# A forgetting-attention and SSD layer: the second query tile's causal mask added by GpSimd, norm sums taken as columns

## The chip, the cores and the metric

The kernel runs on one core of one Trainium2 chip. The metric is device time in microseconds (us), the median of several executions. The engines go by TensorE (PE, its weight loads PEld), VectorE (DVE), ScalarE (ACT), GpSimd (POOL) and SyncE (SP, which issues most transfers). Each takes its instructions in order; they meet at semaphores.

## The reference

One decoder layer for 1024 tokens and 1024 channels in fp32, 16 heads of 64 in either branch:

```
proj = RMSNorm(x) @ w_in -> z_ssm, xBC, dt, q, k, v, f, z_att, g_ssm, g_att
A: xBC -> causal conv, silu -> SSD scan in chunks of 128 -> y
   yg = y * silu(z_ssm);  yg *= rsqrt(mean(yg^2 over the 256 channels of a group) + eps)
B: per head, for each block of 128 queries
   s = q.k / sqrt(64) + F[query] - F[key],   F = cumsum(log sigmoid(f))
   s = -inf where key > query;  o = softmax(s) @ v;  o *= silu(z_att)
merged = sigmoid(g_ssm) * (A @ w_branch_ssm) + sigmoid(g_att) * (B @ w_branch_att)
out = x + RMSNorm(merged @ w_out)
```

Two places matter here: the causal mask in B, and the sum of squares over a group's 256 channels in A.

## The kernel before, in words

Tokens stand in tiles of 128 (`P`), eight of them, in two halves of 512 (`HALF`). The big projections are one long `Stream`: pairs of 128-column units are multiplied in seven products in place of eight (a Strassen-like scheme); every operand is split in a high and a low part so that three fast products make one near fp32. One product into one PSUM bank is 12 matmuls of 512 columns, cut in two half-steps of six. The rest of the program calls `stream.halves(n)` to place half-steps between its own work, so that TensorE has projections to stream while other engines work; a generator that yields n has n half-steps put behind that part (`stream.beside`).

**State-space stage.** `ssd(g)` runs for each of 4 groups over 8 chunks. `squares(g, ch, ...)` takes the norm's sum of squares for half `ch`: both channel tiles are multiplied with the gate, squared by ScalarE, added by VectorE into `zs[0]`. Lines 977 to 991 then split that sum in a high and a low part (`sqp`), let TensorE multiply both with a matrix of ones (`pv`: each row holds the sums of 512 tokens), copy one row (`line`), and turn it in four matmuls into four columns `pc`, which VectorE copies to `rc`. Half 0 is done inside the scan of the same group (`early`, from chunk 4 on), half 1 in `gate_and_norm`, which goes on to take the root, turn `rc` into rows, write them to DRAM (L1012), read them back broadcast as `r` (L1015), scale `xs` (L1022) and store it (L1027).

**Attention.** 8 pairs of heads `hp`, six steps `g` each (`GROUPS`, L1355): query tiles 7, 6 on the far keys and on the near keys, 5, 4 likewise, 3, 2 and 1, 0 on the near keys. In a step `scores(hp, g, u)` runs for both query tiles (u = 0, 1). It makes `s` for both heads e: three products, the heads side by side in the upper and lower half of the array. VectorE's reduction (L1511) writes s + F into `ex` and its minimum (signs are turned) into `nm`; ScalarE's exponential (L1515) works in place and sums up. `turned` then transposes `ex` on TensorE, copies the results to `p` (L1552, L1554), and `weighted` multiplies with v in the next step.

F of the keys is loaded broadcast as `fb` (L1372), for all 128 queries. A diagonal block needs the mask. For the odd query tiles (u = 0) `mask` adds `far`, 1e30 above the diagonal, to 128 columns of `fb` in place, on GpSimd (L1379, two instructions of 64 partitions and 2 x 128 columns). For the even ones (u = 1), whose keys in `fb` the other query tile needs unmasked, TensorE adds it: `corner`, two products with a shifted identity `eye` for either head, at the end of the score block (L1499). A score block of an even tile has 384 or 128 columns, so that in `ex[:, e, 1]` the columns 384 to 511 are unused in those steps; in steps 1 and 3 they hold scores.

The order of pinned instructions (`pin`, `mm`, `turn`) is that of the program, engine by engine; the others are placed by a planner that simulates the program, with `tc.high_priority()` ahead. One pass of the loop at L1691 is one step: scores of both tiles, `weighted` of the step before, half-steps (`ahead`), gates' loads, `loads(m)` (transfers of the coming steps and the masks of `fb`), `turned`, half-steps (`behind`).

Of the kernel before, what the change touches and what calls it, by code (L numbers as in the profile page):

```python
# [8 lines left out]
F32 = mybir.dt.float32  # L9
# [7 lines left out]
P = 128  # L17
# [69 lines left out]
def hybrid_layer(ctx: ExitStack, tc, a, out):  # L87
# [746 lines left out]
    def ssd(g):  # L834
# [108 lines left out]
        for c in range(NT):  # L943
# [11 lines left out]
            if c == 4:  # L955

                z, sq = (sp.tile([P, T + 4], F32, tag="u", bufs=2, name=n) for n in ("z", "sq"))
                sq = sq.bitcast(F32R)
                early = squares(g, 0, [z[:, half(j)] for j in range(2)], [sq[:, half(j)] for j in range(2)], z[0:1, 0:HALF])
                next(early)  # L960
# [5 lines left out]
    def squares(g, ch, zs, sqp, line):  # L966
# [26 lines left out]
    def gate_and_norm(g):  # L993
        xs = [groups[g][f"xs{j}"] for j in range(2)]

        def flat(tag, bufs, name):
            return sp.tile([P, 4, P], F32, tag=tag, bufs=bufs, name=name).rearrange("p a b -> p (a b)")

        yield from squares(
            g, 1, [flat("csb", 2, "z") for _ in range(2)], [flat("m4", 2, "sqp").bitcast(F32R) for _ in range(2)],  # L1000
            flat("ce", 1, "line")[0:1],
        )
# [289 lines left out]
    with tc.tile_pool(name="ssm", bufs=1, reuse_waits="tile", side="right") as sp, tc.tile_pool(  # L1292
        name="ssmp", bufs=1, space=PSUM, reuse_waits="tile", side="right"
    ) as pp:
        onesr = sp.tile([P, P], F32R, name="onesr")
        ones = onesr.bitcast(F32)
# [36 lines left out]
    with tc.tile_pool(name="att", bufs=1, reuse_waits="tile", side="right") as ap, tc.tile_pool(  # L1333
# [8 lines left out]
        nc.vector.memset(big[:, 0:192], -NEG)  # L1342
        for e in range(2):
            nc.vector.tensor_copy(eye[rows[e], 64:P], ident[rows[e], rows[e]])
            nc.gpsimd.affine_select(
                beyond[:, 192 * e : 192 * e + 192], big[:, 0:192], [[1, 192]], ALU.is_gt, 0.0, base=64 * e - 64,
                channel_multiplier=-1,
            )
            nc.vector.tensor_copy(far[rows[e], :], beyond[rows[e], 192 * e : 192 * e + 192])

        corner = [(eye[:, 64:192], far[:, 64:192]), (eye[:, 0:P], far[:, 0:P])]
# [22 lines left out]
        def mask(hp, i):  # L1374

            f = fb[hp, i // 4][:, :, i % 4 * P : i % 4 * P + P]
            for e in range(2):
                c = far[rows[e], 64 - 64 * e : 192 - 64 * e].unsqueeze(1).to_broadcast([64, 2, P])
                pin(nc.gpsimd.tensor_tensor(f[rows[e]], f[rows[e]], c, ALU.add))  # L1379
# [102 lines left out]
        def scores(hp, g, u):  # L1482
# [8 lines left out]
            diagonal = h == i // 4 and u  # L1491
            for m, (x, y) in enumerate(ops):
                for e in range(2):
                    mm(
                        s[e][:, 0:w], x[rows[e]], y[rows[e]], start=(m == 0), stop=(m == 2 and not diagonal),
                        skip_group_check=True,
                    )
            if diagonal:
                for n, (x, y) in enumerate(corner):  # L1499
                    for e in range(2):  # L1500
                        mm(
                            s[e][:, w - P : w], x[rows[e]], y[rows[e]], start=False, stop=(n == 1),
                            skip_group_check=True,
                        )
# [294 lines left out]
```

## Time and profile before

| | |
|---|---|
| runs | 1275.56, 1275.94, 1270.34 us; median 1275.56 |
| the profiled execution | 1276.93 us, span 1275.2 us, mean granted TensorE clock 0.998 |
| busy share of the span | PE 98%, PEld 77%, DVE 80%, ACT 62%, POOL 25% |
| first to last score matmul | 683.7 to 1109.3 us |
| mask matmuls L128 s<-far,eye | 128, 9.8 us busy, 222 ns each (matmuls overlap) |
| masks on GpSimd L1379 | 64, 49.5 us busy |
| norm sums: L977, L984 on ACT, L978 on DVE, pv and pv_t on PE | 8 of each, 16 and 32 matmuls |

A row of the profile gives engine, line, operation, what is written and read (out<-in, buffer numbers left out), partitions x columns and type, and xcount. Matmuls all have L128 and transposes L131, the lines of two helpers: they are told apart by their tiles. L1511 shows as `CUSTOM_DVE_ANT_0` and a short `DVE_READ_ACCUMULATOR2_ANT`, which writes the minimum. Ends of matmuls are modelled, and a matmul's duration (0.39 us for 512 columns) is longer than the distance to the next, so lengths are taken from start to start. In a timeline a row holds neighbouring instructions of one kind, and what stands in square brackets is the engine's idle time before it.

### The profile page before, as it was taken

To read this page: it belongs to the slowest core of one execution; us is meant where nothing else is said; L and a number is where in the kernel's file an instruction comes from. 1 tells how busy PE (TensorE), PEld (TensorE's weight loads), DVE (VectorE), ACT (ScalarE), POOL (GpSimd) and SP (SyncE) were. 2 spreads that over 40 slices of the span, in tenths; PEclk is the share of its full clock that TensorE was granted. 3 is DMA by queue.
4 is the path that set the end of the run, shared out by engine and by line. 5 is a ranking of instruction groups with operands and counts; after the bars stand their busy time and mean duration, and the time that the engine had idled before them with its cause. 6 is when DMAs were issued, how large, how long until landed. Compare 5 with 4: busy or idle time off the path is not lost.

```text
span 1275.2 us, 20797 instructions
## 1 busy us (share of the span) xinstructions
PE 1245.2 (98%) x6912; PEld 981.9 (77%) x6912; DVE 1016.0 (80%) x2001; ACT 793.6 (62%) x1735; POOL 319.5 (25%) x321
## 2 busy tenths in 40 slices
PE   5999999999999999999999999999999999999997
PEld 3688878788888888888887777777777777678886
DVE  7998896888888978997767667767789667797975
ACT  7745665556665765566555666666687666743753
POOL 4000440013400241114102123313112222256062
PEclk9999999999999999999999999999999999999999
DMA  8232452646336533744447576666687657766933
GB/s 294 72 125 73 147 164 87 186 153 195 119 116 206 173 131 111 223 151 134 137 154 255 167 225 200 215 222 217 226 296 273 204 197 244 236 202 212 367 115 100
DMA packets 152235, 233.56 MB, mean 183 GB/s; under 512 B 15200, under 2 KB 60736, under 8 KB 152128
## 3 DMA queue, kind: packets, MB, share of 16 engines
q1 hardware_dynamic: 136064, 196.08, 47.9%
q10 hardware_dynamic: 10560, 18.06, 3.7%
q0 software_dynamic: 5504, 18.09, 3.7%
q8 instruction: 54, 0.88, 0.3%
q14 instruction: 53, 0.43, 0.1%
HBM read 162.99 MB, written 72.34 MB: 185 GB/s over the span
## 4 chain that ended last, share of the span: by engine, by line
PE 80%; DVE 7%; DMA 6%; ACT 4%; issue 2%; SPq 0%; POOL 0%; DVEq 0%; ACTq 0%; POOLq 0%
PE pb L128 33%; PE pc L128 20%; PE pd L128 6%; PE av L128 5%; PE pt L131 5%; PE s L128 5%; PE yps L128 2%; DVE wop L351 1%; DVE sum L356 1%; DMA xt<-in_x 1%; DMA raw<-in_wu 1%; DMA rb<-st_dram 1%; PE st L128 1%; PE tr_v L131 1%; ACT wop L350 1%
## 5 line engine op out<-in xcount | busy, mean ns | idle before, releaser
L350 ACT ACTIVATE wop<-sum 128x512 fp32r<-128x512 f32 x180 | 112.5, 626 | 110.8 <-DVE sum L356 51.2
L351 DVE TENSOR_TENSOR wop<-sum,wop 128x512 fp32r<-128x512 f32 x180 | 137.0, 762 | 53.8 <-ACT wop L350 52.5
L1515 ACT ACTIVATE ex<-ex,nm 128x512 f32<-128x512 f32 (+1 forms) x192 | 116.2, 606 | 75.2 <-DVE nm L1511 74.9
L410 ACT ACTIVATE s<-pb 128x512 f32<-128x512 f32 x143 | 84.7, 592 | 93.4 <-PE pb L128 91.3
L128 PE MATMUL pb<-x0h,wop 128*128 128x512 f32 x384 | 131.6, 399 | 0.0
L351 DVE TENSOR_TENSOR wop<-raw,wop 128x512 fp32r<-128x512 f32 x144 | 106.6, 742 | 31.1 <-ACT wop L350 30.7
L128 PE MATMUL pc<-x2h,wop 128*128 128x512 f32 x384 | 130.3, 398 | 1.1 <-DVE u L425 1.1
L128 PE MATMUL pc<-x3h,wop 128*128 128x512 f32 x384 | 129.8, 396 | 1.1 <-DVE th L423 0.7
L128 PE MATMUL pb<-x4h,wop 128*128 128x512 f32 x384 | 129.1, 395 | 0.0
L128 PE MATMUL pb<-x6h,wop 128*128 128x512 f32 x376 | 126.8, 395 | 1.3 <-ACT s L410 1.3
L128 PE MATMUL pb<-x5h,wop 128*128 128x512 f32 x376 | 127.1, 395 | 0.0
L1511 DVE CUSTOM_DVE_ANT_0 ex<-s,fb 128x512 f32<-128x512 f32 (+1 forms) x192 | 96.8, 552 | 19.9 <-PE s L128 14.6
L350 ACT ACTIVATE wop<-raw 128x512 fp32r<-128x512 f32 x144 | 89.7, 623 | 15.6 <-PE pd L128 6.2
L128 PE MATMUL pd<-x1h,wop 128*128 128x512 f32 x288 | 96.3, 394 | 0.0
L128 PEld LDWEIGHTS pc<-x2h,wop 128*128 128x128 f32 x384 | 72.1, 188 | 18.6 <-issue 2.4
L128 PEld LDWEIGHTS pc<-x3h,wop 128*128 128x128 f32 x384 | 72.1, 188 | 18.2 <-issue 1.6
L128 PEld LDWEIGHTS pb<-x0h,wop 128*128 128x128 f32 x384 | 72.7, 189 | 17.3 <-issue 2.7
L128 PEld LDWEIGHTS pb<-x4h,wop 128*128 128x128 f32 x384 | 72.1, 188 | 16.7 <-issue 1.9
L128 PEld LDWEIGHTS pb<-x6h,wop 128*128 128x128 f32 x376 | 70.6, 188 | 18.1 <-ACT s L410 1.7
L211 POOL TENSOR_TENSOR wd<-wd 128x256 f32<-128x256 f32 x32 | 33.0, 1032 | 202.7 <-DMA wd<-in_wo 138.5
L128 PEld LDWEIGHTS pb<-x5h,wop 128*128 128x128 f32 x376 | 70.6, 188 | 16.7 <-issue 2.0
L128 PE MATMUL pc<-x3l,wop 128*128 128x512 f32 x192 | 75.1, 391 | 1.5 <-DVE x3l L279 1.5
(325 smaller groups left out, 3004.1 us busy)
## 6 DMA issues: line engine op xcount, KB each, us to landing
raw<-in_wu SPq DMA_DIRECT2D x128, 256.0 KB
csb<-cs_dram SPq DMA_DIRECT2D x32, 256.0 KB
q<-q_dram SPq DMA_DIRECT2D x32, 256.0 KB
k<-k_dram SPq DMA_DIRECT2D x16, 512.0 KB
fb<-f_dram SPq DMA_DIRECT2D x16, 512.0 KB
rb<-st_dram SPq DMA_DIRECT2D x48, 128.0 KB
wd<-in_wo SPq DMA_DIRECT2D x40, 128.0 KB
xt<-in_x SPq DMA_DIRECT2D x8, 512.0 KB
```

Of the source, the lines that this page charges most:

```text
L128: return tc.keep_in_program_order(nc.tensor.matmul(*args, **kw))
L131: return tc.keep_in_program_order(nc.tensor.transpose(out_, in_, idn))
L211: pin(nc.gpsimd.tensor_tensor(t[out_], t[a_], t[b_], ALU.subtract))
L350: nc.scalar.activation(op[:, 0], src, AF.Copy)
L351: nc.vector.tensor_tensor(op[:, 1], src, op[:, 0], ALU.subtract)
L356: self.adds.tensor_tensor(t, x, y, ALU.add)
L410: nc.scalar.activation(s, ps, AF.Copy)
L1511: nc.vector.tensor_tensor_reduce(o, s[e][:, 0:w], fb[hp, h][:, e, 0:w], 1.0, 3.0e38, ALU.add, ALU.min, nm)
L1515: pin(nc.scalar.activation(o, o, AF.Exp, scale=-1.0, bias=nm, accum_out=hd.at(hd.sm, i, h, e)))
```

## The change

In the state-space stage the sum of squares is not split. TensorE takes each 128 tokens of `zs[0]` as weights and multiplies a single column of ones, in plain fp32: four matmuls give the four columns at once. The row, its copy, its four turns and one `yield 2` go; so do the tiles for the parts and the row. `ones` is plain fp32.

In the attention `eye`, `corner` and the mask matmuls go. `far` is 128 x 128. `mask` takes one head at a time (128 partitions, 128 columns) and can write its sum elsewhere: for the even query tiles to `spare`, the unused quarter of `ex`. The reduction of tiles 6 and 2 is split in two: all but the last 128 columns against `fb`, then the last 128 against `spare`, starting from the minimum `na` of the first; tiles 4 and 0 have 128 columns only, and take theirs against `spare` in one instruction. The masks for `spare` are issued after `turned` in steps 1 and 3 (for tiles 4 and 2), in `loads` of step 4 (tile 0) and of step 5 (tile 6 of the next heads).

```diff
-    def squares(g, ch, zs, sqp, line):
+    def squares(g, ch, zs):
...
         nc.vector.tensor_tensor(zs[0], zs[0], zs[1], ALU.add)
-        nc.scalar.activation(sqp[0], zs[0], AF.Copy)
-        nc.vector.tensor_tensor(sqp[1], zs[0], sqp[0], ALU.subtract)
         yield 6
-        pv = pp.tile([P, HALF], F32, tag="tr", bufs=2, name="pv")
-        for j in range(2):
-            mm(pv, onesr, sqp[j], start=(j == 0), stop=(j == 1))
-        nc.scalar.activation(line, pv[0:1, :], AF.Copy)
-        yield 2
-        pc = pp.tile([P, HALF], F32, tag="tr", bufs=2, name="pv_t")
+        pc = pp.tile([P, HALF], F32, tag="tr", bufs=2, name="pv")
         for b in range(4):
-            turn(pc[:, b : b + 1], line[:, b * P : (b + 1) * P], ident[0:1, 0:1])
+            mm(pc[:, b : b + 1], zs[0][:, b * P : (b + 1) * P], ones[:, 0:1], start=True, stop=True)
...
-        eye = ap.tile([P, 192], BF16, name="eye")
-        far = ap.tile([P, 192], BF16, name="far")
-        nc.vector.memset(eye, 0.0)
+        far = ap.tile([P, P], BF16, name="far")
         big, beyond = small("big"), small("beyond")
...
-        corner = [(eye[:, 64:192], far[:, 64:192]), (eye[:, 0:P], far[:, 0:P])]
+        nc.vector.memset(big[:, 0:P], -NEG)
+        nc.gpsimd.affine_select(
+            beyond[:, 0:P], big[:, 0:P], [[1, P]], ALU.is_gt, 0.0, base=0, channel_multiplier=-1
+        )
+        nc.vector.tensor_copy(far, beyond[:, 0:P])
...
-        def mask(hp, i):
-            f = fb[hp, i // 4][:, :, i % 4 * P : i % 4 * P + P]
+        def diagonal(hp, i):
+            return fb[hp, i // 4][:, :, i % 4 * P : i % 4 * P + P]
+        spare = ex[:, :, 1, 3 * P : HALF]
+        def mask(hp, i, to=None):
+            f = diagonal(hp, i)
             for e in range(2):
-                c = far[rows[e], 64 - 64 * e : 192 - 64 * e].unsqueeze(1).to_broadcast([64, 2, P])
-                pin(nc.gpsimd.tensor_tensor(f[rows[e]], f[rows[e]], c, ALU.add))
+                pin(nc.gpsimd.tensor_tensor((f if to is None else to)[:, e], f[:, e], far, ALU.add))
...
-            diagonal = h == i // 4 and u
+            apart = w - P if h == i // 4 and u else w
...
-            if diagonal:
-                for n, (x, y) in enumerate(corner):
-                    for e in range(2):
-                        mm(
-                            s[e][:, w - P : w], x[rows[e]], y[rows[e]], start=False, stop=(n == 1),
-                            skip_group_check=True,
-                        )
...
+                least = 3.0e38
                 with tc.high_priority():
-                    pin(
-                        nc.vector.tensor_tensor_reduce(
-                            o, s[e][:, 0:w], fb[hp, h][:, e, 0:w], 1.0, 3.0e38, ALU.add, ALU.min, nm
+                    if apart:
+                        to = nm
+                        if apart < w:
+                            least = to = ap.tile([P, 1], F32, tag=f"na{e}", bufs=1, name="na")
+                        pin(
+                            nc.vector.tensor_tensor_reduce(
+                                o[:, 0:apart], s[e][:, 0:apart], fb[hp, h][:, e, 0:apart], 1.0, 3.0e38, ALU.add,
+                                ALU.min, to,
+                            )
                         )
-                    )
+                    if apart < w:
+                        pin(
+                            nc.vector.tensor_tensor_reduce(
+                                o[:, apart:w], s[e][:, apart:w], spare[:, e], 1.0, least, ALU.add, ALU.min, nm
+                            )
+                        )
...
             if g == 4 and more:
                 mask(hp + 1, 7)
+            if g == 4:
+                mask(hp, 0, spare)
+            if g == 5 and more:
+                mask(hp + 1, 6, spare)
...
         mask(0, 7)
+        mask(0, 6, spare)
...
             made = turned(hp, g, list(end(m - 1)))
+            if g in (1, 3):
+                mask(hp, {1: 4, 3: 2}[g], spare)
```

More of the change, by code (lines that the diff above doesn't have):

```diff
@@ L1294, in hybrid_layer @@
     ) as pp:
-        onesr = sp.tile([P, P], F32R, name="onesr")
-        ones = onesr.bitcast(F32)
+        ones = sp.tile([P, P], F32, name="ones")
         nc.vector.memset(ones, 1.0)
@@ L1494, in scores @@
                     mm(
-                        s[e][:, 0:w], x[rows[e]], y[rows[e]], start=(m == 0), stop=(m == 2 and not diagonal),
+                        s[e][:, 0:w], x[rows[e]], y[rows[e]], start=(m == 0), stop=(m == 2),
                         skip_group_check=True,
                     )
-            if diagonal:
-                for n, (x, y) in enumerate(corner):
-                    for e in range(2):
-                        mm(
-                            s[e][:, w - P : w], x[rows[e]], y[rows[e]], start=False, stop=(n == 1),
-                            skip_group_check=True,
-                        )
             hd = heads[hp]
```

16 lines of the change are left out of this document (3 added, 13 removed).

## The prediction

> **What bounds the kernel now.** First the page: the span, the busy times, the clock, the chain that ended last.
>
> ```profile
> span 1275.2 us, 20797 instructions
> PE 1245.2 (98%) x6912; PEld 981.9 (77%) x6912; DVE 1016.0 (80%) x2001; ACT 793.6 (62%) x1735; POOL 319.5 (25%) x321
> PE 80%; DVE 7%; DMA 6%; ACT 4%; issue 2%; SPq 0%; POOL 0%; DVEq 0%; ACTq 0%; POOLq 0%
> ```
>
> TensorE is busy 98% of the span and makes 80% of the chain. Busy time flatters pipelined matmuls, so I asked next for the attention stage alone (its scores run from 683.7 to 1113 us), and then for what TensorE waited for there. The columns of the stretch are its length and then, by engine, busy us and instructions; those of a wait are us in total, times, longest.
>
> ```profile
> 683.00:1116.00 433.00, 428.65 (x2865) 324.32 (x2863) 321.55 (x849) 293.20 (x741) 109.59 (x144) 1.00 0.67 222
> ```
> ```profile
> PEld s L128 <- ACT p L1554: 8.7, 21, 1.8
> PE pt L131 <- ACT ex L1515: 1.1, 2, 0.9
> ```
>
> TensorE is busy for 428.65 of 433 us at full clock (1.00); VectorE is busy 321.55 us (74%), GpSimd 109.59 us (25%). TensorE's named waits are a few us, nearly all of them for the copies p and not for the exponentials. So in this stage time taken off TensorE is time off the kernel, and time added to VectorE or GpSimd is paid only where it makes TensorE wait.
>
> The first part of the change lies in the state-space stage (about 130 to 683 us), where TensorE's longest wait for VectorE is this one:
>
> ```profile
> PE pc L128 <- DVE u L425: 1.1, 1, 1.1
> ```
>
> It comes once and lasts 1.1 us: little for freed vector time to win.
>
> **The mask matmuls.** 8 head pairs x 4 diagonal score blocks x 4 = 128 matmuls go. What a block costs is read from TensorE's order of time: start, us, instruction, count. The first is a block without mask (12 products of 512 columns), the second has 6 of 512 and 6 of 384, the third 6 of 256 and 6 of 128.
>
> ```profile
> 759.80 1.66 PE L128 MATMUL s<-k,q 64*128 64x512 f32 x12
> 761.39 0.87 PE L128 MATMUL av<-p,v 128*64 128x256 f32 x8
> ...
> 734.20 1.49 PE L128 MATMUL s<-k,q 64*128 64x512 f32 x12
> ...
> 735.74 0.44 PE L128 MATMUL av<-p,v 128*64 128x256 f32 x2
> ...
> 778.42 0.91 PE L128 MATMUL s<-k,q 64*128 64x256 f32 x12
> 779.16 0.30 PE L128 MATMUL s<-far,eye 64*128 64x128 bf16 x4
> 779.39 1.74 PE L128 MATMUL av<-p,v 128*64 128x256 f32 x16
> ```
> ```profile
> 778.42 0.77 PEld L128 LDWEIGHTS s<-k,q 64*128 64x128 f32 x12 [0.35 <-ACT p L1554]
> ```
> ```profile
> 69.09 8.17 PE pb L128 x36
> ```
>
> From its first product to the next stage's first, the block without mask takes 761.39 - 759.80 = 1.59 us. The projections stream 512 columns in 8.17 / 36 = 0.227 us. The two heads of a block run side by side in the halves of the array, so six pairs are 6 x 0.227 = 1.36 us, and 0.23 us is left for the change from this shape to the next. By the same sum the second block without its mask is 0.23 + 3 x 0.227 + 3 x 0.170 = 1.42 us, against 735.74 - 734.20 = 1.54 us now: 0.12 us saved. The third would be 0.23 + 3 x 0.113 + 3 x 0.057 = 0.74 us against 0.97 now, 0.23 saved; but its twelve weight loads alone last 0.77 us, and a last product of 0.057 us stands behind them, which leaves 0.14 saved. I take 0.16, nearer the loads. There are 16 blocks of each kind: 16 x 0.12 + 16 x 0.16 = **4.5 us**. The low end is 16 x 0.12 + 16 x 0.14 = 4.2 us; the high end is the whole stretch from the mask to the next stage, 779.39 - 779.16 = 0.23 us, times 32 = 7.4 us.
>
> [...]
>
> **The split reductions.** Tiles 6 and 2 now reduce 384 columns as 256 and then 128, in 8 x 2 x 2 = 32 places; the second starts from the first one's minimum. Tiles 4 and 0 (128 columns) keep one instruction. VectorE, ScalarE and TensorE in order of time:
>
> ```profile
> 736.79 0.55 DVE L1511 CUSTOM_DVE_ANT_0 ex<-s,fb 128x384 f32<-128x384 f32 x1
> 737.27 0.55 DVE L1511 CUSTOM_DVE_ANT_0 ex<-s,fb 128x384 f32<-128x384 f32 x1
> ...
> 701.80 0.42 DVE L1511 CUSTOM_DVE_ANT_0 ex<-s,fb 128x256 f32<-128x256 f32 x1
> 702.15 0.08 DVE L1511 DVE_READ_ACCUMULATOR2_ANT nm<- 128x1 f32 x1
> ...
> 702.75 0.28 DVE L1511 CUSTOM_DVE_ANT_0 ex<-s,fb 128x128 f32<-128x128 f32 x1
> 702.96 0.29 DVE L1511 CUSTOM_DVE_ANT_0 ex<-s,fb 128x128 f32<-128x128 f32 x1
> ...
> 694.82 0.08 DVE L1511 DVE_READ_ACCUMULATOR2_ANT nm<- 128x1 f32 x1
> 694.94 0.16 DVE L1409 TENSOR_TENSOR nr<-nm 128x4 f32<-128x4 f32 x1
> ```
> ```profile
> 737.73 0.60 ACT L1515 ACTIVATE ex<-ex,nm 128x384 f32<-128x384 f32 x1
> 738.33 0.60 ACT L1515 ACTIVATE ex<-ex,nm 128x384 f32<-128x384 f32 x1
> ```
> ```profile
> 739.40 1.03 PE L131 MATMUL pt<-ident,ex 128*128 128x128 f32 x8
> ```
>
> From start to start, 384 columns take 0.48 us, 256 take 0.35 and 128 take 0.21; an instruction that needs the minimum just written starts 0.12 us behind its reading. So a split place costs 0.08 us more if nothing is waited for, 0.20 us with the wait: 2.6 to 6.4 us of VectorE in all. I take the wait. [...]
>
> Does TensorE see it? In the quoted block the first split place would be done at 736.79 + 0.68 + 0.08 = 737.55 us, and ScalarE is free for it only at 737.73; the second at 738.23, against 738.33. ScalarE's own row of exponentials covers both. Behind it the transposes start at 739.40, 0.47 us after the last exponential, and the eight first ones read the other query tile. Transposes waited for exponentials twice (1.1 us, above); I put 0.2 us on three of the 16 split steps: +0.6 us. If that cover were gone everywhere it would be 2 x 0.2 us in all 16: +6.4 us. Low end: nothing.
>
> **GpSimd's masks.** 64 instructions of 64x256 become 128 of 128x128.
>
> ```profile
> L1379 POOL TENSOR_TENSOR fb<-fb,far 64x256 f32<-64x256 f32 x64 | 49.5, 773 | 75.6 <-DVE nm L1511 45.7 <-ACT ex L1515 13.6 <-DMA raw<-in_wu 5.7
> L895 POOL TENSOR_TENSOR ce<-ce,ct 128x512 f32<-128x512 f32 x28 | 41.9, 1495 | 36.5 <-ACT ce L894 36.5
> ```
>
> 256 columns take 0.773 us and 512 take 1.495: 0.36 us per 128 columns, 0.05 fixed, so 0.41 each and 52 us in all against 49.5. If time went by instructions it would be 0.77 each, 99 us. Either fits an engine that idles 75% of the stage. What matters is order: the copy in the spare quarter has one place, which is free only when the step before is through with it (after tiles 7, 6 and 5, 4 on the far keys: its transposes; else its reductions).
>
> ```profile
> 697.64 1.75 PE pt L131 x16
> ```
> ```profile
> 703.48 0.39 ACT L1515 ACTIVATE ex<-ex,nm 128x128 f32<-128x128 f32 x1
> ```
> ```profile
> 706.43 0.60 PE L131 MATMUL pt<-ident,ex 128*128 128x128 f32 x4
> ```
>
> The transposes end at 699.39; the reduction that reads the copy starts at 702.75. 3.36 us cover two masks of 0.41. Cost: nothing. Queued behind the waiting mask on GpSimd are the stores of the attention's and branches' results, read several steps later.
>
> **The norm sums.** Eight times, two products of 512 columns and four one-row transposes become four fp32 products of one column.
>
> ```profile
> 185.28 0.63 PE L128 MATMUL pv<-sq,onesr 128*128 128x512 f32 x2
> 185.75 0.38 PE L131 MATMUL tr<-ident,xs 128*128 128x128 f32 x2
> 185.97 0.39 PE L128 MATMUL tr<-ct,bt 128*128 128x128 f32 x2
> 186.19 0.60 PE L128 MATMUL st<-xe,bn 128*128 128x256 f32 x2
> ...
> 193.43 0.40 PE L131 MATMUL pv_t<-ident,z 1*128 1x1 f32 x4
> 193.76 0.44 PE L128 MATMUL yps<-m,xdt 128*64 128x128 f32 x4
> ```
>
> Now: 0.47 + 0.33 = 0.80 us. One plain fp32 product is two instructions and takes 186.19 - 185.97 = 0.22 us, so four are 0.88; with one column instead of 128 they may go at a one-row transpose's pace, 0.33 / 4, which makes eight 0.66. Total between 8 x (0.88 - 0.80) = +0.6 and 8 x (0.66 - 0.80) = -1.1 us: I take 0. Two ScalarE copies and a VectorE subtraction per sum go as well, off the path; freeing them can win about the 1.1 us wait above. The columns are ready two half-steps of projections earlier; the transfers behind them (the broadcast of r, the stores) move up SP's queue, past the weight loads, with as much to lose as to win: 0, plus or minus 2 us. The shorter mask constants before the attention cost nothing there: its first scores wait for projections.
>
> **Sum.** -4.5 + 0.6 + 0 + 0 + 0 = -3.9 us. The profiled execution took 1276.93 us, 1.7 us more than its span, and lies 1.4 us above the median of the runs shown, 1275.56: the median goes to 1271.7 us.
>
> **Rivals.** *More than the sum.* Columns at the transposes' pace (-1.1), the wait of the state-space stage gone (-1.1), mask stretch nearer its whole length (-6.5), no late exponentials: -8.7, so 1266.9 us. For it: every term is within its bounds. Against: each must fall on the good side.
>
> *The gain is swallowed.* The waits for copies of p (8.7 us) are met sooner by a TensorE that arrives sooner, and the split reductions push those copies 0.4 us back, so that what the masks free is given to the wait: about 0 to +2, 1275 to 1277 us. For it: 21 such waits. Against: 0.16 us saved on a wait of 0.4 is at most 21 x 0.16 = 3.4.
>
> *The spare quarter comes late; slower.* GpSimd takes its work in order, and these stand in it:
>
> ```profile
> POOL ya_dram L1585 <- DVE zr L1469: 45.7, 5, 12.4
> POOL ms_dram L1083 <- DVE th L1082: 48.3, 10, 9.4
> ```
>
> 15 waits, 6.2 us each. The last exponential of tiles 5 and 4 ends at 703.48 + 0.39, 2.5 us before 706.43, so a mask costs once it is done more than 3.4 + 2.5 = 5.9 us after the transposes; with 0.8 us of masks and a store of 0.5 ahead, once the work that the store waits for is over 4.6 us late. If ten of the 15 stood ahead of a mask for their full length, each would cost 6.2 + 1.3 - 5.9 = 1.6 us: +16 - 4 = +12, 1287 us; half of it 1280. Against: what those stores wait for was mostly written ahead of the mask, so it is done by then.
>
> **How the numbers follow.** Forecast (1268 to 1274): 0.52; more than the sum (1263 to 1268): 0.20; swallowed (1274 to 1278): 0.16; the late quarter (1279 to 1288): 0.12. A measurement of this kernel can tell about 0.5%, 6.4 us, from no change: faster means below 1269.2, slower above 1281.9. Faster takes the second case and 0.08 of the forecast's low end, 0.28; slower takes 0.09 of the last; 0.63 is the same. 1264 to 1279 leaves out the last case and the tail of the second.
>
> **What would show it.** The masked blocks should shrink to about 1.42 and 0.81 us from first product to next stage; the 32 split places should read 256 and then 128 columns 0.47 us apart; masks at 0.41 us; no wait of VectorE's reduction for GpSimd; TensorE's waits for ex and p no longer than now. A reduction waiting for the spare quarter, or gaps ahead of the transposes in the split steps, would make the forecast wrong; norm products at much over 0.9 us a sum would too.

## The result: 11 us slower, and the profile after

The changed kernel takes 1286.26 us in the median of 6 runs (1284.92 to 1288.65), the kernel before 1274.95 us (6 runs on the same chip, 1270.34 to 1276.81). The ratio is 1.0094, with a 95% interval of 1.0074 to 1.0114. The forecast was 1271.7 us, the range 1264 to 1279. The profiled execution is the one of 1288.65 us, the slowest of the six.

First the page of the changed kernel: span, busy times, the chain that ended last by engine.

```profile
span 1286.6 us, 20828 instructions
PE 1246.2 (97%) x6800; PEld 984.9 (77%) x6800; DVE 1015.6 (79%) x2053; ACT 790.0 (61%) x1719; POOL 329.5 (26%) x384
...
PE 80%; DVE 8%; DMA 4%; ACT 4%; issue 3%; SPq 1%; POOL 0%; DVEq 0%; ACTq 0%; POOLq 0%
```

112 matmuls fewer (6800 against 6912), and TensorE's busy time still rises from 1245.2 to 1246.2 us. Shorter work that is not less busy is a first hint that some of it ran slower.

Where do the 11.4 us of span (1286.6 - 1275.2) arise? The timelines of TensorE give the start of the attention's scores and its last product with v, first of the kernel before, then of the changed one.

```profile
683.68 1.50 PE L128 MATMUL s<-k,q 64*128 64x512 f32 x12
...
1120.08 0.87 PE L128 MATMUL av<-p,v 128*64 128x256 f32 x8
```
```profile
680.78 1.49 PE L128 MATMUL s<-k,q 64*128 64x512 f32 x12
...
1130.98 0.87 PE L128 MATMUL av<-p,v 128*64 128x256 f32 x8
```

Ahead of the attention the changed kernel is 2.9 us in front. The attention takes 450.2 us instead of 436.4: 13.8 us more. What follows it is within 0.5 us of the same. So the loss is in the attention, and it is larger than the result shows. The scores themselves did become shorter, by the same timeline of the changed kernel:

```profile
699.90 0.91 PE L128 MATMUL s<-k,q 64*128 64x256 f32 x12
700.74 1.95 PE L128 MATMUL av<-p,v 128*64 128x256 f32 x16
...
716.23 1.49 PE L128 MATMUL s<-k,q 64*128 64x512 f32 x12
717.65 1.95 PE L128 MATMUL av<-p,v 128*64 128x256 f32 x16
```

The block of 384 columns takes 717.65 - 716.23 = 1.42 us (1.54 before), that of 128 columns 0.84 (0.97 before): 16 x 0.12 + 16 x 0.13 = 4.0 us are freed. TensorE's waits in the attention (us in total, times, longest) show what took their place:

```profile
PE pt L131 <- DVE nm L1501: 10.8, 10, 3.0
PE pc L128 <- DVE x3l L279: 1.6, 1, 1.6
PE pt L131 <- ACT ex L1505: 1.4, 3, 0.7
```

L1501 is the second half of the split reduction (and the one reduction of tiles 4 and 0). The transposes wait for it ten times, 10.8 us, always in the steps of tiles 6 and 2. Before, the transposes' only waits of any size were 1.1 us. The place with the longest wait, in order of time (start, us; in brackets the idle time ahead):

```profile
953.62 0.41 DVE L1494 CUSTOM_DVE_ANT_0 ex<-s,fb 128x256 f32<-128x256 f32 x1
953.96 0.08 DVE L1494 DVE_READ_ACCUMULATOR2_ANT na<- 128x1 f32 x1
953.96 0.68 DVE L279 TENSOR_TENSOR x5l<-x5l,x5h 128x512 fp32r<-128x512 f32 x1
954.57 0.68 DVE L1448 TENSOR_TENSOR o<-av,zr 128x512 f32<-128x512 f32 x1
955.17 0.68 DVE L1590 TENSOR_TENSOR x<-zr,x 128x512 f32<-128x512 f32 x1
955.77 0.34 DVE L1501 CUSTOM_DVE_ANT_0 ex<-s,ex,na 128x128 f32<-128x128 f32 x1
956.15 0.61 ACT L1505 ACTIVATE ex<-ex,nm 128x384 f32<-128x384 f32 x1
956.26 0.45 PE L131 MATMUL pt<-ident,ex 128*128 128x128 f32 x1 [2.98 <-DVE nm L1501]
...
958.68 1.30 PE L131 MATMUL pt<-ident,ex 128*128 128x128 f32 x5 [1.98 <-DVE nm L1501]
...
719.16 0.42 DVE L1494 CUSTOM_DVE_ANT_0 ex<-s,fb 128x256 f32<-128x256 f32 x1
719.51 0.08 DVE L1494 DVE_READ_ACCUMULATOR2_ANT na<- 128x1 f32 x1
719.73 0.35 DVE L1501 CUSTOM_DVE_ANT_0 ex<-s,ex,na 128x128 f32<-128x128 f32 x1
```

The reader should look at what stands between L1494 and L1501. In the lower place there is nothing: 0.14 us pass from the end of the reading to the second half. In the upper one three other VectorE instructions of 0.68 us stand there, and the second half begins 1.73 us after the first one's minimum is read. The second half must wait for that minimum, and the planner, which simulates this wait, has filled it with whatever was ready. In the order of VectorE's instructions 15 of the 32 split places are filled, with 25 instructions by the trace (the expectations below give 24, the count in the plan). The 32 gaps from the reading to the second half add up to 16.9 us. The ten waits of the transposes lie in six steps, each with at least one filled place.

How does this reach TensorE? Not through ScalarE. At 956.26 us the transposes go on 0.11 us after the exponential of the late block has begun, and that takes 0.61 us. In head pair 2 they go on before it has begun:

```profile
792.01 1.14 PE L131 MATMUL pt<-ident,ex 128*128 128x128 f32 x5 [0.55 <-DVE nm L1501]
...
792.66 0.60 ACT L1505 ACTIVATE ex<-ex,nm 128x384 f32<-128x384 f32 x1
```

In all ten places the transposes go on 0.22 or 0.23 us after VectorE begins to read the minimum of L1501, with that block's own exponential still running or yet to come. They belong to the other query tile, whose exponentials are there. The program shows what they lack: score blocks `s` and transposes `pt` take turns in the same four PSUM tiles (tag `s`, `bufs=4`, L1472 and L1516). Two of the four were those of the other query tile and are free, so two transposes run; the third needs the tile out of which the first head's second half is still reading, the fourth that of the second head (956.26 and 958.68 us above). No run gave `pt` tiles of its own; the times and the program are what shows it.

The rest is the clock. The table of windows (length; busy us and instructions of PE, PEld, DVE, ACT, POOL; granted clock; DMA share; GB/s), for the three stretches of half clock in the attention and the stretch ahead of each:

```profile
788.79:792.20 3.41, 1.69 (x10) 1.11 (x9) 2.93 (x8) 1.36 (x6) 2.22 (x4) 1.00 0.65 199
792.20:795.61 3.41, 3.41 (x15) 2.91 (x14) 1.38 (x2) 2.88 (x8) 0.00 (x0) 0.50 0.37 129
952.59:956.00 3.41, 0.44 (x2) 0.20 (x2) 3.41 (x8) 3.41 (x9) 0.54 (x1) 1.00 1.05 410
956.00:962.83 6.83, 4.59 (x17) 3.98 (x18) 5.09 (x13) 4.05 (x11) 1.08 (x2) 0.50 0.98 374
1123.29:1126.70 3.41, 1.53 (x10) 0.79 (x7) 2.54 (x9) 3.37 (x10) 0.00 (x0) 1.00 0.84 272
1126.70:1130.11 3.41, 3.41 (x8) 2.73 (x9) 3.41 (x7) 1.94 (x5) 0.54 (x1) 0.50 0.31 120
```

The kernel before has no such stretch in its attention. TensorE worked for 3.41 + 4.59 + 3.41 = 11.41 us at half clock. In the last of these stretches products of 512 columns start 0.43 us apart, against the 0.227 of the forecast's row, so up to half of it, 5.7 us, is lost; less where TensorE would have waited behind it anyway. Together: -4.0 (blocks) + 10.8 (waits for L1501) + 0.3 (waits for exponentials, 1.4 against 1.1) + at most 5.7 (clock) = at most 12.8 of the 13.8 us.

### The profile page after: what moved, and what is told of

It reads as the page before. It is cut to its first block, busy times and chain, and to the rows that moved or that the text cites. A ratio compares the mean times of both kernels' runs of the same rounds, so it can differ in the third digit from the quotient of the medians.

```text
span 1286.6 us, 20828 instructions
## 1 busy us (share of the span) xinstructions
PE 1246.2 (97%) x6800; PEld 984.9 (77%) x6800; DVE 1015.6 (79%) x2053; ACT 790.0 (61%) x1719; POOL 329.5 (26%) x384
## 4 chain that ended last, share of the span: by engine, by line
PE 80%; DVE 8%; DMA 4%; ACT 4%; issue 3%; SPq 1%; POOL 0%; DVEq 0%; ACTq 0%; POOLq 0%
PE pb L128 34%; PE pc L128 20%; PE pd L128 6%; PE pt L131 5%; PE av L128 4%; PE s L128 4%; PE yps L128 2%; DVE wop L351 1%; DMA raw<-in_wu 1%; PE st L128 1%; DVE ex L1494 1%; DMA xt<-in_x 1%; PE tr L131 1%; ACT wop L350 1%; PE tr_v L131 1%
## 5 line engine op out<-in xcount | busy, mean ns | idle before, releaser
L351 DVE TENSOR_TENSOR wop<-sum,wop 128x512 fp32r<-128x512 f32 x180 | 140.6, 783 | 51.5 <-ACT wop L350 50.7
L351 DVE TENSOR_TENSOR wop<-raw,wop 128x512 fp32r<-128x512 f32 x144 | 105.0, 730 | 26.8 <-ACT wop L350 25.3
L1494 DVE CUSTOM_DVE_ANT_0 ex<-s,fb 128x512 f32<-128x512 f32 (+1 forms) x160 | 86.8, 578 | 21.7 <-PE s L128 19.6
L131 PE MATMUL pt<-ident,ex 128*128 128x128 f32 x576 | 79.8, 280 | 12.9 <-DVE nm L1501 10.8
L131 PEld LDWEIGHTS pt<-ident,ex 128*128 128x128 f32 x576 | 68.3, 144 | 24.4 <-issue 7.5
```

Of the source, the lines that this page charges most:

```text
L131: return tc.keep_in_program_order(nc.tensor.transpose(out_, in_, idn))
L351: nc.vector.tensor_tensor(op[:, 1], src, op[:, 0], ALU.subtract)
L1494: nc.vector.tensor_tensor_reduce(o[:, 0:apart], s[e][:, 0:apart], fb[hp, h][:, e, 0:apart], 1.0, 3.0e38, ALU.add, ALU.min, to,)
```

## The experiments

The theory at the outset: the split reductions make the exponentials late, since other VectorE work gets between their halves. The rivals: the copy in the spare quarter, which GpSimd writes, comes late; the norm sums upset the order of the work; the masked blocks were worth nothing. The first four runs part these, the next three ask what is left once the wait is gone, the last five ask about the clock.

### The norm sums alone

Only the state-space part of the change; the attention as before.

```diff
-    mm(pv, onesr, sqp[j]) ...; activation(line, pv[0:1, :]); turn(pc[:, b : b + 1], line ...)
+    mm(pc[:, b : b + 1], zs[0][:, b * P : (b + 1) * P], ones[:, 0:1])
```

> The kernel before with the norm sums as columns, and nothing of the mask's change. Theory W: the loss sits in the attention, where the second half of a split reduction needs the minimum of the first, so that the planner puts other VectorE work between the two, exponentials and transposes come late, and TensorE stands and then runs at a lower clock. By W the norm part alone is worth what the first score shows in the changed kernel, 680.8 against 683.7 us: about -3 us, 1272. Rival P: any edit reshuffles the plan, and the attention suffers whatever is changed; then this one loses too, 1278 or more.

1273.59 us against 1275.57, ratio 0.9983 (0.9968 to 0.9998). The norm sums are not the loss; they win about 2.2 us. In its trace the first scores start at 680.8 us, 2.9 us earlier than before, as in the changed kernel.

### The mask part alone

The whole change of the attention, with the norm sums as before.

```diff
-    mm(pc[:, b : b + 1], zs[0][:, b * P : (b + 1) * P], ones[:, 0:1])
+    mm(pv, onesr, sqp[j]) ...; activation(line, pv[0:1, :]); turn(pc[:, b : b + 1], line ...)
```

> The changed kernel with the norm sums as before. W: the attention's loss stays (from first score to the last product with v it is 13.8 us longer than before), without the 2.9 us won ahead of it: 1289 us. Rival P: another plan, and the loss shrinks to a few us: 1275 to 1280.

1288.45 us, ratio 1.0106 (1.0089 to 1.0123). The loss is all in the attention's part, and the rival of the norm sums falls.

### The halves of both heads interleaved

```diff
-for e: reduce(e, first half, na[e]); reduce(e, second half, from na[e])
+for e: reduce(e, first half, na[e])
+for e: reduce(e, second half, from na[e])
```

> The changed kernel, but the four reductions of a split block go first half of head 0, first half of head 1, second half of head 0, second half of head 1: same instructions, one other between the two that depend on each other. In the plan other work now stands ahead of a second half at 10 places with 16 instructions in all, against 15 places with 24. W: the waits are met once in place of twice, so about half of the attention's loss of 18 us (13.8 and the 4.5 that the mask matmuls free) goes: 1277 us, with transposes' waits for minima down from 10.8 to some 5 us. Rival C, it is the count of reductions and not their dependence: 1286, no change. Rival G, the masks in the spare quarter come late: 1286 too.

1281.35 us, ratio 1.0054 (1.0034 to 1.0074). With the other head's half in the wait, 10 places instead of 15 are filled, with 17 instructions instead of 25, and TensorE's waits for the second half fall from 10.8 to 7.5 us. Some four tenths of the loss go (the ratio falls by 0.0040 of 0.0094); half was expected, 1277 us, with waits of some 5 us. So the direction fits the theory and the size is missed: other work still stands ahead of a second half in 10 places.

### Split reductions in the kernel before

```diff
-reduce(ex[0:384], s + fb, nm)
+reduce(ex[0:256], s + fb, nm)
+reduce(ex[256:384], s + fb, starting from nm, nm)
```

Mask matmuls, masks and norm sums are those of the kernel before; no spare quarter.

> The kernel before, mask matmuls and all, with the reductions of tiles 6 and 2 split in 256 and 128 columns, the second starting from the first's minimum; no spare quarter, no masks more on GpSimd. W: nearly the whole loss without the gain: 1275 + 18 = 1293, less where a late TensorE gives cover: 1288 to 1293. Rival G (spare quarter late) and rival E (TensorE comes earlier than its partners once the mask matmuls are gone): the split alone is hidden, 1275 to 1279.

1288.85 us, ratio 1.0111 (1.0089 to 1.0134). The split alone is as slow as the whole change, again with 15 places filled by 25 instructions, and with stretches of half clock at 959.9 and 1130.5 us. The rival of the spare quarter falls as the main cause: there is none here. The run of the mask part alone, which has the split and frees the 4.0 us of the mask matmuls, is not clear of this one (1.0106, 1.0089 to 1.0123); why the 4.0 us do not show between the two was not tried.

### The second half no longer waits for the first

```diff
-least = to = na
+to = na        # the second half starts from 3.0e38; its minimum alone is nm
```

This changes the shift of the exponentials in tiles 6 and 2: it is taken over the last 128 keys alone, and the first half's minimum is not used. The softmax is the same as long as the exponentials stay in range.

> The changed kernel, but the second half of a split reduction starts from a constant and alone gives the value that the exponentials subtract; the first half's minimum is not read. So the largest logit that is subtracted is that of the last 128 keys and not of all 384, which shifts numerator and denominator of the softmax alike. Same instructions and columns, no wait of one reduction for the other; in the plan no other work stands between two halves (24 instructions before). W: the whole attention loss goes, and what the norm (-2.9) and the mask matmuls (-4.5) free is left: 1268 us (1266 to 1271), transposes' waits for minima under 2 us. Rival C, the 32 reductions more and their slower form: 1284 to 1286. Rival G, the spare quarter late: 1284 to 1286.

1276.38 us against 1273.64, ratio 1.0019 (1.0005 to 1.0032). No place is filled any more. The ratio falls by 0.0075 from the changed kernel's 1.0094, 9.6 us, with the same number of VectorE instructions, the same masks and the same spare quarter; only the dependence is gone. But the expected 1266 to 1271 us were not reached. TensorE's waits and the windows of this kernel show what is left:

```profile
PE pt L131 <- ACT ex L1505: 2.6, 2, 1.8
...
PE pt L131 <- DVE nm L1501: 0.8, 2, 0.5
```
```profile
946.67:950.08 3.41, 1.86 (x10) 1.06 (x10) 3.41 (x13) 3.41 (x10) 0.02 (x1) 1.00 1.00 367
950.08:956.91 6.83, 5.46 (x19) 4.13 (x21) 4.28 (x8) 3.73 (x10) 1.59 (x3) 0.50 0.97 352
1110.51:1113.92 3.41, 1.26 (x9) 0.79 (x7) 1.79 (x5) 2.94 (x8) 0.00 (x0) 1.00 0.73 259
1113.92:1117.34 3.42, 3.27 (x8) 2.59 (x9) 3.42 (x8) 1.96 (x5) 0.54 (x1) 0.50 0.13 51
```

The transposes' waits are down to 3.4 us in all, yet up to (5.46 + 3.27) / 2 = 4.4 us still go to the clock, in head pairs 5 and 7 as in the changed kernel.

### The spare quarter written and not read

```diff
-apart = w - P if h == i // 4 and u else w
+apart = w                        # one reduction against fb
```

GpSimd still writes its masks into the spare quarter, and nobody reads them there. The even query tiles are left without a mask, so the kernel leaves out a part of the computation.

> The changed kernel with one reduction in each place and F as loaded: GpSimd still writes the spare quarter, nothing reads it, so the even query tiles are left without a mask. It gives the price of the mask matmuls and what the split costs even without its wait. W: 1268 us, as the run without the start value, or 0.5 us less. If the mask matmuls were hidden anyway (rival E): 1272, as with the norm sums alone.

1269.8 us, ratio 0.9970 (0.9958 to 0.9981). No stretch of half clock. Mask matmuls gone, GpSimd's masks all written, reductions unchanged: this is the forecast's sum without the split. 1268 us were expected, and 1272 if the mask matmuls had been hidden; 1269.8 lies between. In the attention the gain is there: from the first scores to the last product with v it takes 431.2 us, against 435.0 with the norm sums alone. Writing the masks costs nothing that shows; waiting for those in the spare quarter is not in this run, since nobody reads them. Set against the kernel with independent halves, it is faster in the two places where that one has half clock: from the first scores of head pair 5 to those of pair 6 it takes 57.4 us against 60.4, and from those of pair 7 to the last product with v 60.7 against 62.8. These 5.1 us are more than the whole difference of the two profiled spans, 1270.1 and 1273.7 us.

### Spare quarter for the short tiles only

Tiles 4 and 0 read the spare quarter, tiles 6 and 2 keep mask matmuls and one reduction; masks in the old shape of 64x256; norm sums as columns.

```diff
-diagonal = h == i // 4 and u
+diagonal = h == i // 4 and u and w > P
+f = spare if h == i // 4 and u and w == P else fb[hp, h]
```

> Norm sums as columns; masks in the spare quarter for tiles 4 and 0 alone (128 columns, one reduction), mask matmuls kept for tiles 6 and 2; no split anywhere. W: -2.9 - 16 x 0.16 = -5.5, 1270 us. Rival G, a mask in the spare quarter comes late: 1275 or more. Rival E, the matmuls were hidden: 1272.

1274.0 us, ratio 0.9998 (0.9982 to 1.0014): no gain over the norm sums alone, where 2 us were expected. VectorE's waits show one price that the other kernels hardly pay, the second line:

```profile
DVE ex L1502 <- POOL fb L1369: 3.7, 2, 2.4
DVE ex L1502 <- POOL ex L1369: 3.3, 3, 2.1
```

The old shape takes two instructions of 0.77 us (the row of before) for one mask. With it the rival of the late quarter does occur, in small; in the changed kernel the same waits are 2.0 and 0.4 us, and in the kernel before, which has no spare quarter, the first is 5.0. But this does not explain the missing gain. The profiled execution took 1280.27 us, the slowest of the 12, with half clock from 952.7 us (3.4 us) and from 1116.6 us (6.8 us). Its head pairs 0 to 4 together are 1.8 us shorter than with the norm sums alone; pairs 5 and 7, where the half clock lies, are 1.5 and some 4 us longer. What the median execution lost is not shown.

### Both ways, by head pair

The kernel with independent halves, but in head pairs 5 and 7 the mask again as a matrix product (128 rows, one for each head) and one reduction.

```diff
+diagonal = h == i // 4 and u and hp in (5, 7)
+if diagonal: mm(s[e][:, w - P : w], eye, far)        # eye: 128 x 128
```

> e5_no_start with the mask as matrix products again (one product of 128 rows for each half of the heads instead of two of 64) and one reduction in the head pairs 5 and 7, the two in which its clock was halved; everywhere else GpSimd's sums and the independent halves. The shift of the exponentials in the even tiles of the other head pairs is again the smallest sum of the last 128 keys alone. Where it keeps up: by head pair 5 e5 was 5.0 us ahead of the kernel before against 3.4 us for e1_norm_only, and head pairs 0 to 4 and 6 gain 0.13 us a block. Theory 'the halved clock is what e5 lost': no stretch of half clock in head pair 5 or at the end, a span of 1269.5 (e1's 1271.4 less 1.5 to 2) and a time of 1271.5 us, 0.995 to 0.998 of before. Rival 'e5 lost it to the lateness of the sums by GpSimd or the halves themselves, whatever the clock': the gain of head pairs 0 to 4 is given back, 1274 us.

1268.79 us against 1274.35, ratio 0.9954 (0.9939 to 0.9969). Faster than either kernel, with the shift of the exponentials restricted as in the kernel with independent halves. The ratio lies within the expected 0.995 to 0.998, though the profiled execution again has a stretch of half clock in head pair 5, where none was expected. So the loss of the kernel with independent halves is mended, but not in the way that the expectation said. 3.3 us of the gain over the norm sums alone are won in head pair 7 of the profiled executions (58.6 us from its first scores to the last product with v, against 61.9); why there was not tried.

### One late instruction, long and short

The kernel with the norm sums alone, which has no half clock, with one VectorE instruction more, ahead of the reductions of tile 6 in the first step of head pair 5. What it writes is overwritten.

```diff
+if (hp, g, u, e) == (5, 0, 1, 0):
+    tensor_reduce(ex[:, 0, 1, 511:512], fb repeated n times, min)      # n = 5, or 1
 tensor_tensor_reduce(ex, s, fb, ...)
```

> e1_norm_only (mask products, one reduction, no half clock) with one more VectorE instruction at one place: a reduction of 5 x 512 elements, about 2.7 us by 0.53 us for 512 columns, ahead of the reductions of the second query tile in step 0 of head pair 5. It has nothing to do with masks; what it computes is overwritten. The stall of TensorE in the transposes there, 1.9 us in e1, grows to about 4.5 us. Theory 'a stall of about 4 us costs a halved clock': a stretch of 6.8 us at half clock begins within 10 us of it, head pair 5 becomes 2.7 + 3.4 = 6 us longer than e1's 56.8, a time of 1279 us. Rival 'the half clock comes with the change's plan and not with a stall': no stretch, head pair 5 2.7 us longer at most, 1276 us.

> As e9_late_5 with 512 elements instead of 2560: 0.53 us more at that one place, a stall of about 2.4 us. Theory 'a stall of about 4 us costs a halved clock, one of 2.9 us does not': no stretch of half clock in head pair 5, which becomes 0.5 us longer than e1's 56.8; 1274 us. Rival 'any delay at that place is multiplied': 2 us or more longer, 1276 us.

The long one: 1278.8 us, ratio 1.0025 (1.0005 to 1.0044). Its instruction took 2.82 us, 0.56 for each 512 elements, and is TensorE's wait of 2.9 us; the windows around it:

```profile
954.75:958.16 3.41, 0.96 (x6) 0.55 (x4) 3.41 (x4) 3.01 (x7) 0.54 (x1) 1.00 0.81 301
958.16:961.57 3.41, 2.98 (x14) 2.60 (x14) 3.41 (x9) 3.04 (x10) 0.46 (x1) 0.51 0.92 321
```

Head pair 5 takes 61.6 us against 56.8: 4.8, of which the clock can be 2.98 / 2 = 1.5 here and 1.7 in a second stretch of the same pair, from 985.5 us, which was not expected. (This execution lost further time ahead of the attention, where the kernel is the same; pair 5 alone is read.) Here TensorE's wait for VectorE alone, 2.9 us in a kernel that has no split and no spare quarter, was followed by a clock of 0.51.

The short one was to show that the 0.53 us expected of it bring none. It did not: 1275.25 us, ratio 1.0007 (0.9992 to 1.0021), head pair 5 1.6 us longer, with a stretch of half clock behind a stall of 2.3 us in two pieces. The kernel with the unused spare quarter stalls for 2.2 us at this place and keeps its clock. So the length of the stall does not decide, and my theory that about 4 us are needed falls.

### The same two kernels again

What does decide? In all 14 profiles all changes of the clock within one execution lie a whole number of 3.413 us apart: in the changed kernel's 792.2, 956.0 and 1126.7 us are 48 and 50 such steps from one another. The grid does not lie at the same place in every execution: 792.2 us in the changed kernel's and 950.08 us in that of the kernel with independent halves are 46.25 steps apart.

> The kernel of e8_both_ways once more, unchanged, for its time against the kernel before on another occasion and for a second profiled execution. In the traces so far all stretches of half clock of one execution begin on one grid of 3.413 us (in the changed kernel's profile at 232, 280, 330 and 376 steps of it), the grid lies elsewhere in each execution, and a stretch follows a step of the grid in which TensorE ran matrix products for about half of the time or less. Theory 'the grid decides': the time again 0.994 to 0.997 of before, some 1268 to 1270 us; in head pair 5 the stall of 1.1 us in the transposes is the same to 0.5 us, and whether a stretch of half clock follows it depends on where the grid lies, so it can be absent this time. Rival 'a stall at this place always costs the clock': the stretch at 950 us is there again.

> The kernel of e10_late_1 once more, unchanged: a stall of 2.3 us in two pieces (0.7 and 1.5 us) in head pair 5, after which the clock was halved for 3.4 us in the first profile. Theory 'the grid decides': the executions fall into two groups about 2 us apart, around 1273 and 1276 us, and the half clock in head pair 5 is there if a step of the grid holds both pieces of the stall, and absent if they fall into different steps, with the length of the stall the same to 0.5 us. Rival 'the length decides': the stretch is there again, the times lie around one middle.

The first again took 1269.0 us against 1274.66, ratio 0.9954 (0.9942 to 0.9967). Its second profile has no half clock in the attention. Windows of the first execution on its grid and the waits of the transposes there, then the same for the second execution:

```profile
947.12:950.53 3.41, 1.97 (x13) 1.18 (x12) 3.41 (x9) 3.41 (x10) 0.68 (x2) 1.00 1.03 372
950.53:953.95 3.42, 3.42 (x13) 2.38 (x12) 3.42 (x6) 3.08 (x8) 0.94 (x2) 0.50 0.99 279
```
```profile
947.57 0.33 PE L131 MATMUL pt<-ident,ex 128*128 128x128 f32 x1 [0.33 <-DVE nm L1501]
...
950.21 1.08 PE L131 MATMUL pt<-ident,ex 128*128 128x128 f32 x5 [0.79 <-ACT ex L1512]
```
```profile
947.16:950.57 3.41, 2.45 (x16) 1.84 (x15) 2.34 (x5) 3.41 (x10) 1.07 (x2) 1.00 1.02 390
950.57:953.99 3.42, 2.97 (x22) 1.80 (x22) 3.42 (x7) 1.94 (x6) 0.54 (x1) 1.00 0.97 340
```
```profile
946.47 0.33 PE L131 MATMUL pt<-ident,ex 128*128 128x128 f32 x1 [0.31 <-DVE nm L1501]
...
949.11 0.77 PE L131 MATMUL pt<-ident,ex 128*128 128x128 f32 x5 [0.79 <-ACT ex L1512]
```

The same program, the same waits to 0.02 us, but in the second execution they come 1.1 us earlier on a grid that lies within 0.04 us of the first one's. The step of the grid then holds 2.45 us of matrix work instead of 1.97, and the clock stays whole. The rival, that a stall at this place always costs the clock, falls.

The pair also gives a price for the half clock itself, and it is small here: head pair 5 takes 57.5 us with it and 57.4 without. In the second execution TensorE waits 0.45 us for VectorE at 951.7 us, where the slower first one has no wait of that size. So half of a stretch's work is an upper bound of what it costs.

The short late instruction again: 1275.57 us, ratio 1.0013 (0.9999 to 1.0026). The half clock is there again in head pair 5, as both theories allow, since the step from 950.25 to 953.66 us holds nearly all of both pieces of the stall. Its 12 times lie between 1272.5 and 1280.8 us without the two groups that the theory of the grid had expected, so this run does not tell the theories apart.

## Why the prediction was wrong, point by point

**What bounds the kernel** held. TensorE set the time in the attention of the kernel before (busy for 428.65 of 433 us), and the change then made it wait, 10.8 us for L1501. (The last score matmul starts at 1109.3 us, not at the 1113 given there; nothing hangs on it.)

**The mask matmuls** held. Blocks of 1.42 us were forecast and measured; 0.81 for the short ones against 0.84. That the 0.23 us left over in the unmasked block stay in the others was an estimate, which the 1.42 us of the longer block bear out; what takes them no run shows. The 4.5 us were 4.0, and in the kernel with the unused spare quarter the attention is 3.8 us shorter than with the norm sums alone. Of the whole time 1.7 us show there (ratios of 0.9970 and 0.9983, whose intervals overlap): in its trace the attention starts 1.3 us later and what follows it takes 1.2 us more.

**The split reductions** is the step that failed, at two points. The first is "I take the wait", which priced the second half's wait for the minimum at 0.12 us, from two neighbouring rows, as if nothing could come between. In 17 of the 32 places nothing does: the second half begins 0.22 us after the reading begins (0.12, as priced, in the kernel with the split alone; why 0.1 more here was not tried) and takes 0.346 us, where a reduction from a constant takes 0.285. In the other 15 the planner used the wait for other VectorE work, and the second half began up to 2.3 us after the end of the reading. The rows to ask for were in the trace of before: VectorE has such instructions of about 0.7 us (L1463, which is L1448 in the changed kernel, L279, L351) all through the stage, and the planner that places them stands in the description of the kernel.

The second is the answer to "Does TensorE see it?", that "ScalarE's own row of exponentials covers both". It followed the lateness through the exponentials alone, and noted that the first eight transposes read the other query tile, as if these were safe. It is those that wait: the third needs the PSUM tile that a late second half still reads, and no queue of ScalarE's covers that. Where no other work came between, nothing was late enough to show. And the upper bound, +6.4 us, was worked out from 0.2 us a place and so was no bound: the waits for L1501 are 10.8 us.

**GpSimd's masks** held in effect and missed in size.

```profile
L1364 POOL TENSOR_TENSOR ex<-fb,far 128x128 f32<-128x128 f32 x64 | 33.9, 549 | 82.5 <-PE pt L131 63.4 <-DVE nm L1501 11.0 <-ACT p L1544 8.0
L1364 POOL TENSOR_TENSOR fb<-fb,far 128x128 f32<-128x128 f32 x64 | 30.5, 494 | 52.0 <-DVE na L1494 30.9 <-DVE nm L1494 20.6 <-DMA q<-q_dram 0.3
```

They take 0.55 and 0.49 us instead of 0.41, 64 us instead of 52. GpSimd was free, and it shows no cost: in the changed kernel VectorE's reductions waited 2.4 us for it, in the kernel before 5.0.

**The norm sums** were taken at 0 and win 2.2 us by the runs (0.3 to 4.1 by the interval of the ratio), 2.9 in the trace. 1.6 us of these come between 194 and 295 us, where TensorE's wait of 1.1 us for u is no longer there. The products themselves are as priced, between the bounds: 0.82 us from the first to the next work, against 0.80.

**The rivals.** "More than the sum" (1266.9 us, a ratio of 0.9932) was reached by no run. The kernel with the unused spare quarter has the forecast's own ratio (1271.7 / 1275.56 = 0.9970), but not for its reasons: the norm sums, taken at 0 there, make 2.2 of its 3.8 us by the runs. That the two agree is luck. "The gain is swallowed" named the right place (VectorE pushed back, TensorE waiting) but the wrong products, the copies p, and stopped at +2. "The spare quarter comes late" gave the right size, 1280 to 1287 us, for a reason that the rows exclude. What was missing is a rival by which an instruction that must wait is overtaken, and one by which a stalled TensorE loses its clock.

**The clock** was in no step. It is up to 5.7 of the 13.8 us lost in the attention. The stretch that the prediction shows is at 1.00, and nothing in it could have priced a fall; but a full clock in the kernel before was no promise for a kernel with longer stalls.

## What to carry to other kernels

A split into two dependent parts can cost more than both parts (here 32 gaps of 16.9 us in all stood between them): where something else orders the work, the wait between them is an open slot, and the second part is as late as the work that is put there. Make the parts independent, or price the split with the neighbours' durations in the gap. Ask of a late instruction not only who reads its result but also what it holds on to: here it was the PSUM tile that TensorE's next work needed. And count stalls of TensorE as possibly more than their length: here the 3.4 or 6.8 us behind some of them ran at a clock of 0.50, which can cost up to half of the work in them, while the same stall was followed by half clock in one execution and not in another.

## What the runs showed of the hardware that was not expected

**The clock changed in steps of 3.413 us, mostly after a step with little matrix work.** In all 14 profiles the half clock began on a grid of 3.413 us, and between 150 and 1250 us it lasted one step or two. There all 14 steps in which TensorE ran matmuls for less than 0.46 of the time were followed by half clock, none of those with more than 0.78; between these, both occurred (0.48 was not followed by it in the kernel with short tiles, 0.58 was in the first execution shown above, 0.72 was not in the second, 0.74 was in the kernel with interleaved halves). So the share alone does not decide. Windows of the kernel before, which kept its clock:

```profile
953.70:957.10 3.40, 2.68 (x14) 1.91 (x16) 3.40 (x6) 3.40 (x10) 0.88 (x2) 1.00 1.00 340
1114.07:1117.48 3.41, 1.86 (x12) 1.19 (x11) 2.55 (x7) 3.41 (x9) 0.00 (x0) 1.00 0.82 260
1117.48:1120.89 3.41, 3.41 (x20) 2.08 (x18) 3.41 (x6) 2.08 (x6) 0.54 (x1) 1.00 0.19 75
```

In the step from 1114.07 us the kernel before ran matmuls for 1.86 us, a share of 0.55, and kept its clock, with less matrix work than the 1.97 us that half clock followed in the first execution shown above. Whether that work is transposes does not settle it. The step of 1.97 us that was followed by half clock held transposes alone, and in the step of 1.86 us at 1114.07 us, which was not, 1.08 us were transposes. But the step of 1.98 us ahead of the half clock at 985.5 us, in the kernel with the long late instruction, and that of 2.54 us ahead of 1112.5 us in the kernel with interleaved halves held none. What does is open.

**A reduction that starts from a value in memory took longer than one that starts from a constant**: 0.346 us against 0.285 us for 128 columns, 32 of each in the changed kernel (0.348 against 0.285 in the kernel with the split alone).

```profile
L1501 DVE CUSTOM_DVE_ANT_0 ex<-s,ex,na 128x128 f32<-128x128 f32 x32 | 11.1, 346 | 2.5
L1501 DVE CUSTOM_DVE_ANT_0 ex<-s,ex 128x128 f32<-128x128 f32 x32 | 8.4, 285 | 0.5 <-POOL ex L1364 0.4
```
